# A two-layer streaming encoder on one core: another written order for TensorE (constants' products later, q k products two chunks ahead, samples' keys loaded early)

## The chip, the cores and the metric

The kernel runs on one core of one Trainium2 chip. The metric is the device time of one execution in microseconds (us). Engines are named as the profile names them: PE is TensorE (PEld its weight loads), DVE VectorE, ACT ScalarE, POOL GpSimd, SP the engine that issues the DMAs. L12 is line 12 of the kernel's file; where the change shifts lines, a line of the kernel before is meant unless the text says otherwise.

## What is computed

Two layers over 512 prompt frames (one stream) and 8 x 16 sample frames of running streams. Cut to what matters here:

```
def _hybrid_layer(x, ...):
    proj = _rms_norm(x, norm1) @ w_in          # u_a, g_a, u_b, q, k, v
    out_a = _rglru_mixer(u_a, g_a, ...)        # conv of width 4, two gates, scan
    out_b = _s5_mixer(u_b, ...)                # complex state space, scan
    q, k = _rope(q), _rope(k)
    out_c = _swa_prompt(q, k, v, sinks)        # prompt: chunks of 64, window of 3 chunks
          # or _swa_cached(q, k, v, cache_k, cache_v, sinks) for the samples
    x = x + concat([out_a, out_b, out_c]) @ w_out
    return x + square(relu(_rms_norm(x, norm2) @ w_up)) @ w_down
```

Attention is 8 heads of 64 on 2 heads of keys; its softmax has a sink logit per head.

## The kernel before

The 640 columns (frames) are two groups g of 320: 256 prompt frames (four chunks cq of 64) and 64 sample frames. Products with the large weights come in units of 128 output rows: 8 blocks of 128 x 128, in two halves of 4. In the first projection (layer 0, g = 0) the weights are used as they are (L271, 8 products a unit); everywhere else a weight is split in two parts on ACT (L243) and DVE (L244), and a half is 12 products (L274, L275, L276).

Three mixers run beside these products, for each layer and group: LRU ("L"), S5 ("S") and attention ("A"). Each is a Python generator; a string TURNS says whose turn is next, and `weave(M, n, A, m)` writes n turns of the mixers between m halves of products. So the order on PE is written out by hand, in the order in which Python calls it. The orders on DVE, ACT, POOL and SP are made when the program is built, by a scheduler that simulates the program; each engine then runs its list in order.

PSUM banks come from small pools: three for the large products ("mm"), two for attention and the LRU's gates ("att"), two for S5 ("s5"), one for norms ("fin"). A tile of a pool waits until the tile that had its place has been read for the last time.

The places that the prediction's steps touch:

- The start: products on zeros (L1156), the first input's norm (`first(0)`, with L374 and L411 on PE), then the constants of S5: `lru_const` and `s5_small` (L429 to L515, small DVE operations), `s5_const` with complex products on DVE and POOL (L520 to L526) into the tile tab, transposes of tab on PE (L176, into banks s), products L570, and tables by doubling (L589 to L611).
- S5: transposes of ub, copies L808 and L815, products with B (L822), evacuation against the tables (L829), scan (L840), then products L855, L858 and at last L886.
- LRU: conv (L750), gates (L759 on PE, L760 on ACT), scans (L776), the product with the gate (L781 and L782 on POOL).
- Attention: `own` transposes the samples' values (L176, att<-vS; copied by L921), `sprobs` has the samples' q k products (L952) and their softmax, `sturned` transposes these probabilities, `svalues` (L970) multiplies them with the values. `probs(cq)` has a chunk's q k products (L994) and softmax, `turned` the transposes, `values` the products with the values (L1015).
- `soft`: row maxima (L929), exponentials on ACT (L935), scaling on DVE and POOL (L945). `sprobs` and `probs` each take both att banks and give them back when the exponentials are done.

Of the kernel before, what the change touches and what calls it, by code (L numbers as in the profile page):

```python
# [14 lines left out]
AF = mybir.ActivationFunctionType  # L15
# [132 lines left out]
def encoder_kernel(ctx: ExitStack, tc: tile.TileContext, a, o):  # L148
    nc = tc.nc
    PE, V, S, G = nc.tensor, nc.vector, nc.scalar, nc.gpsimd  # L150
    mm = PE.matmul
    tt = V.tensor_tensor
    act = S.activation
# [20 lines left out]
    def transpose(out, in_):  # L174
        n = in_.shape[0]
        PE.transpose(out, in_, ident[0:n, 0:n])  # L176

    def bigr():
        return big.tile([128, 8, 2, NG], F32R, tag="big", name="bigr")
# [20 lines left out]
    W, n = {}, 0  # L200
# [16 lines left out]
    tab = cst.tile([128, 3840], F32, name="tab")  # L217
# [104 lines left out]
    def weave(steps, n, fill, m):  # L322

        done = 0
        for i in range(n):
            next(steps, None)
            while done < (i + 1) * m // n:
                next(fill, None)
                done += 1
# [563 lines left out]
            dma(o["send"][L], P["send"])  # L893


    def attention(L, P, g, q, mix, c):
        c, mix = c(), mix()

        kcT, p = c.at(0, 2, 2, 144), [c.at(640 + 288 * n, 2, 144) for n in range(2)]
# [2 lines left out]
        half = [slice(32 * n, 32 * n + 16) for n in range(2)]  # L902
        vn, pn = ([c.at(o, 2, 128)[h] for h in half] for o in (1792, 2048))

        pes = [c.at(640 * n, 2, 320) for n in range(2)]
        PTs = [c.at(1280 + 512 * n, 2, 256) for n in range(2)]
        kT, vt = kvs[L]["kT"], kvs[L]["vt"]

        def loads():
            for hf in range(2):  # L910
                dma(kcT[:, hf, :, 0:128], a["kc"][L, 2 * g + hf])
                dma(vc[:, hf], a["vc"][L, 2 * g + hf])
            gcopy(kcT[:, :, :, 128:144], q.kS.rearrange("p (h b t) -> p h b t", t=16, h=2))

        def own():
            b = bank3("att", 4, 128)[0:16]
            for hf in range(2):
                for i in range(2):
                    transpose(b[:, 2 * hf + i], q.vS[:, 16 * (2 * hf + i):16 * (2 * hf + i) + 16])
            for hf in range(2):  # L920
                V.tensor_copy(vn[hf], b[:, 2 * hf:2 * hf + 2])  # L921
# [25 lines left out]
        def sprobs():  # L947
            bs = [bank3("att", 2, 256) for hf in range(2)]
            for hf, b in enumerate(bs):
                for i in range(2):  # L950
                    for kv in range(2):
                        mm(b[64 * kv:64 * kv + 64, i, 0:144], lhsT=q.qS[64 * kv:64 * kv + 64, 2 * hf + i].rearrange("p i t -> p (i t)"),  # L952
                           rhs=kcT[64 * kv:64 * kv + 64, hf, i], start=True, stop=True)
            soft([b[:, :, 0:144] for b in bs], p, sks[:, L:L + 1], nsks[:, L:L + 1], True)
# [27 lines left out]
        def probs(cq):  # L982
            j, kts, nk, k0, st, w0 = geo(cq)
            q0 = 64 * cq
            if cq == 0:
                for pe in pes:
                    G.memset(pe[:, :, 0:64], 0.0)
                    G.memset(pe[:, :, 256:320], 0.0)
            bs = [bank3("att", 2, 256) for kv in range(2)]
            for pr in range(2):  # L990
                for s in range(2):
                    for kv, b in enumerate(bs):
                        ps = slice(64 * kv, 64 * kv + 64)
                        mm(b[64 * s:64 * s + 64, pr, 0:nk], lhsT=q.q[ps, 2 * pr + s, q0:q0 + 64], rhs=kT[ps, k0:k0 + nk], start=True, stop=True)  # L994
            soft([b[:, :, 0:nk] for b in bs], [pe[:, :, st:256] for pe in pes], skp[:, L], nskp[:, L], False)

        def turned(cq, kv):
            j, kts, nk, k0, st, w0 = geo(cq)
            b = bank("att").rearrange("p (t n q) -> p t n q", t=2, n=2)
            for kt in kts:  # L1000
                for n in range(2):
                    transpose(b[:, kt, n], pes[kv][:, n, w0 + 128 * kt:w0 + 128 * kt + 128])
            t0 = kts[0]
            src = b[:, t0:2].rearrange("p t n q -> p t (n q)")
            if kv == 0:
                act(PTs[kv][:, t0:2], src, AF.Copy)
            else:
                V.tensor_copy(PTs[kv][:, t0:2], src)

        def values(cq):  # L1010
            j, kts, nk, k0, st, w0 = geo(cq)
            b = bank("att")[:, 0:256]
            for kv in range(2):
                for kt in kts:
                    mm(b[64 * kv:64 * kv + 64, :], lhsT=vt[:, j - 1 + kt, 64 * kv:64 * kv + 64], rhs=PTs[kv][:, kt],  # L1015
                       start=kt == kts[0], stop=kt == 1)
            src = b.rearrange("p (i q) -> p i q", i=4)
            q0 = 64 * cq
            act(mix[:, 4:8, 0, q0:q0 + 64], src, AF.Copy)
            tt(mix[:, 4:8, 1, q0:q0 + 64], src, mix[:, 4:8, 0, q0:q0 + 64].bitcast(F32), OP.subtract)  # L1020

        loads()
        own()
        yield
        sprobs()
        yield
        sturned(0)
        yield
# [2 lines left out]
        svalues(0)  # L1031
        svalues(1)
        yield
        probs(0)
        for cq in range(4):
            yield
            for kv in range(2):
                turned(cq, kv)
            yield
            if cq < 3:  # L1040
                probs(cq + 1)
                yield
            values(cq)


    TURNS = "LSSLSSSS" "LAAAAAAA" + 5 * "AAS"

    def mixers(L, P, g, q, out, scratch=None):
        c = Carve(bigf() if scratch is None else scratch)
        mix = []  # L1050

        def gens(n):
            if not mix:
                mix.append(bigr())
            return mix[0]

        out["mix"] = gens
        ca = []

        def catt():  # L1060
            if not ca:
                ca.append(Carve(tp.tile([128, 2304], F32, tag="att", name="att")))
            return ca[0]

        G3 = {"L": lru(L, P, g, q, lambda: gens(0), c), "S": s5(L, P, g, q, lambda: gens(0), c),
              "A": attention(L, P, g, q, lambda: gens(0), catt)}
        for t in TURNS:
            next(G3[t], None)
            yield
        for v in G3.values():  # L1070
            assert next(v, "end") == "end"
# [77 lines left out]
    ctx.enter_context(tc.manual_schedule(engines={mybir.EngineType.PE}))  # L1149

    warm = bank("fin")
    zr = bigr()[:, 0:1].rearrange("p a b c -> p (a b c)")
    G.memset(tab[:, 512:1152], 0.0)
    act(zr, tab[:, 512:1152], AF.Copy)
    for n in 8 * (512,) + 4 * (512, 384):
        mm(warm[:, 0:n], lhsT=zr[:, 0:128], rhs=zr[:, 0:n], start=True, stop=True)  # L1156
    dma(sm[:, 0:80], a["sm"][:, 0:80])
    raws = first(0)
    P = {}
    q, m = [Proj(), Proj()], [{}, {}]  # L1160
    A = stream(in_proj(0, 0, norms[0], q[0], raws))
    weave(iter(()), 1, A, 4)
    dma(sm[:, 80:], a["sm"][:, 80:])
    first(1)
    small_prep()
    s5_small(lru_const())
    small = layer_small(0, P)
    next(small)
    weave(small, 2, A, 10)
    M = mixers(0, P, 0, q[0], m[0], setup[0])  # L1170
    weave(M, 8, A, 10)
    run(A)
    for L in range(DEPTH):
        last = L == DEPTH - 1
        A = stream(in_proj(L, 1, norms[1], q[1]))
        weave(M, 23 if L == 0 else 8, A, 16)
        run(M)
        M = mixers(L, P, 1, q[1], m[1])
        weave(M, 8, A, 8)
        run(A)  # L1180
        hm = {}
        F = stream(out_proj(L, 0, m[0], hm))
        weave(M, 7, F, 16)
        run(F)
        F = stream(mlp(L, 0, (0,), hm, fresh=(0,)))
        weave(M, 16, F, 28)
        run(M, F)
        run(stream(out_proj(L, 1, m[1], hm)))
        run(stream(mlp(L, 0, (1,), hm, fresh=(1,))))
        run(stream(mlp(L, 1, (0, 1), hm)))  # L1190
        run(stream(mlp(L, 2, (0, 1), hm)))
        nxt = (lambda g: Norm(g, None)) if last else (lambda g: Norm(g, n1(L + 1)))
        norms = {}
        F = stream(mlp(L, 3, (0,), hm, nxt, norms))
        if last:
            run(F)
            end = [norms[0].flush, lambda: finals(0)]
            items = mlp(L, 3, (1,), hm, nxt, norms)
            items[3:3] = end[:1]
            items[5:5] = end[1:]  # L1200
            run(stream(items))
        else:
            P = {}
            small = layer_small(L + 1, P)
            next(small)
            weave(small, 2, F, 24)
            run(F)
            q, m = [Proj(), Proj()], [{}, {}]
            A = stream(in_proj(L + 1, 0, norms[0], q[0]))
            weave(iter(()), 1, A, 14)  # L1210
            M = mixers(L + 1, P, 0, q[0], m[0])
            weave(M, 8, A, 10)
            run(A)
            F = stream(mlp(L, 3, (1,), hm, nxt, norms))
            weave(M, 15, F, 32)
            run(F)
# [27 lines left out]
```

## Time and profile before

| | |
|---|---|
| three runs | 1485.14, 1485.28, 1489.25 us (median 1485.28) |
| profiled execution | 1489.39 us, its span 1487.6 us |
| PE busy | 1377.3 us, 93% of the span |
| PE idle | 110.3 us |
| mean granted clock of PE | 0.959 of full speed |
| DVE, ACT, POOL busy | 881.3, 653.7, 356.0 us |

Busy times are sums over one profiled execution. A view with idle times names in brackets what ended them; when the engine named had finished long before, it was another. The 1.8 us between span and time lie outside of the profile's first and last instruction.

### The profile page before, as it was taken

What the parts mean: (1) busy time and instruction counts of PE and PEld (TensorE: products, weight loads), DVE (VectorE), ACT (ScalarE), POOL (GpSimd) and SP (SyncE); (2) the same over time, 40 slices, a digit from 0 to 9 for tenths busy, and PEclk for the clock granted to TensorE, in tenths of its full rate; (3) what the DMA queues carried; (4) which work ended last, traced back from release to release, by engine and by line L of the source; (5) the groups of instructions that cost most, each with busy time, mean ns of one, the idle gap of its engine ahead of it and who ended that gap; (6) DMA issues with size and microseconds to landing.
All of it is one profiled execution on the core that took longest, in us unless ns stands there. A gap on an engine that the chain in (4) does not pass through costs nothing.

```text
span 1487.6 us, 25403 instructions
## 1 busy us (share of the span) xinstructions
PE 1377.3 (93%) x9436; PEld 1315.2 (88%) x9436; DVE 881.3 (59%) x1726; ACT 653.7 (44%) x1348; POOL 356.0 (24%) x566
## 2 busy tenths in 40 slices
PE   4596896999999999999997999799999999999997
PEld 3465785989999999999996899699999999999997
DVE  7666677766644334336777677776664433434574
ACT  4155574545533223224575567654543322323543
POOL 4553248251101001006433223421100100100111
PEclk8796997999999999999998999899999999999998
DMA  6131232335432222224432333233443222223452
GB/s 214 38 111 36 68 116 81 98 118 163 143 128 71 80 78 71 77 87 128 144 117 79 104 119 117 83 106 114 147 144 122 71 72 80 77 71 107 149 177 93
DMA packets 91387, 156.24 MB, mean 105 GB/s; under 512 B 14336, under 2 KB 18304, under 8 KB 91264
## 3 DMA queue, kind: packets, MB, share of 16 engines
q1 hardware_dynamic: 91264, 154.63, 31.6%
q8 instruction: 74, 1.21, 0.3%
q14 instruction: 49, 0.40, 0.1%
HBM read 151.02 MB, written 3.37 MB: 104 GB/s over the span
## 4 chain that ended last, share of the span: by engine, by line
PE 85%; POOL 5%; DVE 4%; ACT 2%; issue 2%; DMA 1%; SPq 0%; DVEq 0%; POOLq 0%; ACTq 0%
PE mm L274 25%; PE mm L275 25%; PE mm L276 25%; PE mm L271 3%; PE att L176 1%; PE att L1015 1%; PE fin L411 1%; PE att L994 1%; PE s L176 1%; PE s L858 1%; PE s L886 1%; PE att L970 1%; DVE wl L244 1%; PE fin L374 1%; DMA raw<-w_in 1%
## 5 line engine op out<-in xcount | busy, mean ns | idle before, releaser
L274 PE MATMUL mm<-bigr,wh 128*128 128x320 f32 x2592 | 822.4, 317 | 2.3 <-POOL bigr L156 2.3
L275 PE MATMUL mm<-bigr,wh 128*128 128x320 f32 x2592 | 808.4, 312 | 0.9 <-DVE bigr L1091 0.9
L276 PE MATMUL mm<-bigr,wl 128*128 128x320 f32 x2592 | 808.0, 312 | 0.0
L243 ACT ACTIVATE wh<-raw 128x512 fp32r<-128x512 f32 x520 | 327.2, 631 | 517.6 <-PE mm L275 484.6
L274 PEld LDWEIGHTS mm<-bigr,wh 128*128 128x128 f32 x2592 | 494.3, 191 | 15.8 <-issue 8.3
L275 PEld LDWEIGHTS mm<-bigr,wh 128*128 128x128 f32 x2592 | 494.4, 191 | 2.2 <-DVE bigr L1091 1.3
L276 PEld LDWEIGHTS mm<-bigr,wl 128*128 128x128 f32 x2592 | 493.8, 190 | 0.0
L244 DVE TENSOR_TENSOR wl<-raw,wh 128x512 fp32r<-128x512 f32 x520 | 375.7, 723 | 179.8 <-ACT wh L243 168.4
L156 POOL TENSOR_SCALAR bigr<-t 128x320 fp32r<-128x320 f32 x128 | 59.7, 467 | 662.9 <-ACT t L1089 662.9
L1075 DVE TENSOR_TENSOR xT<-xT,mm 128x320 f32<-128x320 f32 x160 | 77.9, 487 | 133.6 <-PE mm L276 133.5
L1088 DVE SCALAR_TENSOR_TENSOR t<-mm,r 128x320 f32<-128x320 f32 x128 | 62.5, 491 | 94.2 <-PE mm L276 93.9
L1091 DVE TENSOR_TENSOR bigr<-t,bigr 128x320 fp32r<-128x320 f32 x128 | 66.0, 515 | 74.7 <-POOL bigr L156 74.6
L1089 ACT ACTIVATE t<-t 128x320 f32<-128x320 f32 x128 | 60.1, 472 | 111.0 <-DVE t L1088 105.3
L368 POOL TENSOR_TENSOR ss<-ss,sq 128x320 f32<-128x320 f32 x58 | 55.7, 960 | 184.5 <-ACT sq L361 178.8
L176 PE MATMUL att<-ident,att 128*128 128x128 f32 (+1 forms) x144 | 23.7, 301 | 40.9 <-DVE att L945 35.6
L176 PEld LDWEIGHTS att<-ident,att 128*128 128x128 f32 (+1 forms) x144 | 16.8, 143 | 44.9 <-issue 31.0
L945 POOL TENSOR_SCALAR att<-att,st 128x192 f32<-128x192 f32 (+3 forms) x40 | 33.0, 832 | 67.9 <-ACT wh L243 45.7
L935 ACT ACTIVATE att<-att,st 128x192 f32<-128x192 f32 (+3 forms) x80 | 30.6, 395 | 27.3 <-DVE st L933 20.9
L361 ACT ACTIVATE sq<-xT 128x320 f32<-128x320 f32 x66 | 30.5, 462 | 17.7 <-POOL ss L368 10.7
L348 ACT ACTIVATE bigr<-xT,sm 128x320 fp32r<-128x320 f32 x56 | 30.6, 561 | 11.3 <-DVE xT L1075 9.1
L690 POOL TENSOR_TENSOR sw<-sw,cs 128x320 f32<-128x320 f32 x20 | 17.5, 874 | 70.5 <-ACT sw L689 54.9
L349 DVE SCALAR_TENSOR_TENSOR bigr<-xT,sm,bigr 128x320 fp32r<-128x320 f32 x56 | 34.0, 615 | 0.5 <-ACT bigr L348 0.3
(291 smaller groups left out, 1070.2 us busy)
## 6 DMA issues: line engine op xcount, KB each, us to landing
raw<-w_up SPq DMA_DIRECT2D x192, 256.0 KB, 2.6
raw<-w_down SPq DMA_DIRECT2D x192, 256.0 KB, 2.6
raw<-w_in SPq DMA_DIRECT2D x85, 256.0 KB, 2.7
raw<-w_out SPq DMA_DIRECT2D x64, 256.0 KB, 2.6
wl<-w_in SPq DMA_DIRECT2D x11, 256.0 KB, 2.9
xT<-x SPq DMA_DIRECT2D x8, 320.0 KB, 5.7
yT<-xT SPq DMA_DIRECT2D x8, 320.0 KB, 2.9
cs<-rope SPq DMA_DIRECT2D x4, 320.0 KB, 3.3
```

The source lines that it names most:

```text
L156: return G.tensor_scalar(out, in_, 1.0, 0.0, OP.mult, OP.add)
L176: PE.transpose(out, in_, ident[0:n, 0:n])
L243: act(h, raw, AF.Copy)
L244: tt(l, raw, h.bitcast(F32), OP.subtract)
L274: mm(pt, lhsT=h[:, k % 4], rhs=m[:, k, 0], start=k == 0, stop=False)
L275: mm(pt, lhsT=h[:, k % 4], rhs=m[:, k, 1], start=False, stop=False)
L276: mm(pt, lhsT=l[:, k % 4], rhs=m[:, k, 0], start=False, stop=k == 7)
L368: G.tensor_tensor(self.ss, self.ss, sq, OP.add)
L1075: tt(xT[:, g, k], xT[:, g, k], pt, OP.add)
L1088: V.scalar_tensor_tensor(t, pt, 0.0, norm.r, OP.max, OP.mult)
L1089: act(t, t, AF.Square)
L1091: tt(am[:, f, 1], t, am[:, f, 0].bitcast(F32), OP.subtract)
```

## The change

It writes another order for PE, in five edits.

1. The start: 12 products of 128 x 128 on the zeroed tile Mm take the place of 16 products on a zeroed tile of their own. Only one unit is written ahead of the constants instead of two units; 15 more halves follow before the constants' transposes, and the second group's norm (`first(1)`) moves behind the constants.
2. Mixers of layer 0, g = 0: 9 turns between 4 halves instead of 8 between 10.
3. Attention: `loads` becomes a turn of its own and the first of all (TURNS now begins with A). `probs(0)` stands before `sturned(0)`, `probs(1)` behind `svalues`, and then a chunk's transposes come two chunks behind its q k products.
4. Two sets of probabilities (`sets`): chunks 0 and 2 use words 3200 to 4480 of the mixers' scratch tile, chunks 1 and 3 the old place. The LRU's x2 and t2 lie in the words 3200 to 4528 of the same tile.
5. TURNS and the counts of `weave` are fitted to the one turn more.

```diff
-    def attention(L, P, g, q, mix, c):
+    def attention(L, P, g, q, mix, c, cs):
...
-        pes = [c.at(640 * n, 2, 320) for n in range(2)]
+
+        sets = [[cs.at(3200 + 640 * n, 2, 320) for n in range(2)], [c.at(640 * n, 2, 320) for n in range(2)]]
...
-            if cq == 0:
+            pes = sets[cq % 2]
+            if cq < 2:
...
-                    transpose(b[:, kt, n], pes[kv][:, n, w0 + 128 * kt:w0 + 128 * kt + 128])
+                    transpose(b[:, kt, n], sets[cq % 2][kv][:, n, w0 + 128 * kt:w0 + 128 * kt + 128])
...
+        def turn(cq):
+            for kv in range(2):
+                turned(cq, kv)
+
         loads()
+        yield
         own()
         yield
         sprobs()
+        yield
+        probs(0)
         yield
         sturned(0)
...
-        probs(0)
+        probs(1)
+        yield
         for cq in range(4):
+            turn(cq)
             yield
-            for kv in range(2):
-                turned(cq, kv)
-            yield
-            if cq < 3:
-                probs(cq + 1)
+            if cq < 2:
+                probs(cq + 2)
                 yield
             values(cq)
-
-
-    TURNS = "LSSLSSSS" "LAAAAAAA" + 5 * "AAS"
+            yield
+
+
+    TURNS = "ALSSLSSSS" "LAAAAAA" + 5 * "SAA" + "A"
...
-    weave(iter(()), 1, A, 4)
+    weave(iter(()), 1, A, 2)
     dma(sm[:, 80:], a["sm"][:, 80:])
-    first(1)
     small_prep()
     s5_small(lru_const())
     small = layer_small(0, P)
     next(small)
-    weave(small, 2, A, 10)
+    first(1)
+    weave(iter(()), 1, A, 15)
+    weave(small, 2, A, 3)
     M = mixers(0, P, 0, q[0], m[0], setup[0])
-    weave(M, 8, A, 10)
+    weave(M, 9, A, 4)
```

On PE, at the start of the program, the transposes of tab (the constants) stand as follows in the difference; the products between (L271) are left out where they are many.

```order
 L271 MATMUL mm<-bigf,wl 128x320 x4
-L176 MATMUL s_386<-ident,tab 128x128 x4
-L176 MATMUL s_392<-ident,tab 128x128 x4
 L411 MATMUL fin<-ident,rsq 128x128 x2
 L411 MATMUL fin<-ident,rsq 128x64
...
+L176 MATMUL s_536<-ident,tab 128x128 x4
+L176 MATMUL s_542<-ident,tab 128x128 x4
+L271 MATMUL mm<-bigf,wl 128x320 x4
+L570 MATMUL s_575<-tab 128x32 x8
```

Before, they stood ahead of L411 and of 80 of the first projection's 96 products; now 68 of these 96 stand ahead of them: 16, then 44 in one run behind L411, then, behind the transposes of v, 8 more.

On DVE, in the same stretch of the changed kernel, the evacuations of the first projection stand between the last steps of the constants (t and kT belong to k, the t of L672 to v):

```order
L526 TENSOR_TENSOR tab<-tab 128x256
L699 TENSOR_TENSOR t<-mm,cs 128x320
L520 TENSOR_TENSOR tab<-s5s,tab 128x256
L525 TENSOR_TENSOR tab<-s5s,tab 128x256
L522 TENSOR_TENSOR tab<-tab 128x16x16
L700 TENSOR_TENSOR kT<-t,sw 128x256
L701 TENSOR_TENSOR kS<-t,sw 128x64
```

Before, all of the constants' steps stood ahead of L699.

On PE, in the first mixers' attention, the part from the samples' q k products to the transposes of their probabilities, in the difference (what is left out are products L274 to L276):

```order
-L952 MATMUL att<-att,qS 64x144 x8
...
+L953 MATMUL att<-att,qS 64x144 x8
...
+L996 MATMUL att<-kT,q 64x64 x8
 L176 MATMUL att<-ident,att 128x128
 L176 MATMUL att<-ident,att 16x128
```

The q k products of chunk 0 (L996, before L994) came to stand between the two. Before, 12 products stood between L952 and the transposes in this pass; in the later three passes 24. Now 12 stand before L996 and none behind it in this pass; in layer 1, g = 0, 24 and 24; in the two passes of g = 1, 24 and 36.

## Rows read from the trace of the kernel before

**Rows 1.** The profile's page: busy time of each engine, share of the span, instructions.

```profile
PE 1377.3 (93%) x9436; PEld 1315.2 (88%) x9436; DVE 881.3 (59%) x1726; ACT 653.7 (44%) x1348; POOL 356.0 (24%) x566
```

**Rows 2.** Waits of PE: line, awaited; us in total, times, longest.

```profile
PE att L176 <- DVE att L945: 35.6, 6, 10.7
PE s L176 <- DVE tab L522: 27.2, 1, 27.2
PE att L952 <- issue: 10.3, 3, 5.5
```

**Rows 3.** A window of 50 us: busy time of PE, PEld, DVE, ACT, POOL; clock, DMA.

```profile
400.00:450.00 50.00, 50.00 (x343) 50.00 (x342) 26.92 (x45) 18.03 (x30) 2.90 (x7) 1.00 0.39 127
```

**Rows 4.** PE in time, layer 0: start, duration, what, [idle before].

```profile
52.44 1.94 PE L176 MATMUL s<-ident,tab 128*128 128x128 f32 x8 [27.20 <-DVE tab L522]
...
61.19 2.32 PE L271 MATMUL mm<-bigf,raw 128*128 128x320 f32 x8
63.34 2.32 PE L271 MATMUL mm<-bigf,wl 128*128 128x320 f32 x8
...
67.65 1.87 PE L570 MATMUL s<-tab 128*128 128x32 f32 x16
...
102.73 1.11 PE L822 MATMUL s<-bigf,Bm 64*128 64x80 f32 x14 [0.66 <-DVE bigf L829]
...
113.95 1.01 PE L176 MATMUL att<-ident,vS 128*16 128x128 f32 x4 [4.49 <-ACT bigf L760]
```

**Rows 5.** DVE in time, start of layer 0.

```profile
36.26 0.84 DVE L525 TENSOR_TENSOR tab<-s5s,tab 128x256 f32<-128x256 f32 x1
...
49.49 0.42 DVE L525 TENSOR_TENSOR tab<-s5s,tab 128x256 f32<-128x256 f32 x1
...
62.41 3.10 DVE L750 SCALAR_TENSOR_TENSOR bigf<-uap,sm,bigf 128x332 f32<-128x332 f32 x6 [9.15 <-ACT bigf L748]
69.91 0.19 DVE L590 TENSOR_TENSOR tab<-tab 128x16 f32<-128x16 f32 x1 [4.39 <-POOL tab L156]
...
84.49 0.83 DVE L609 COPY tab<-s5s 128x1280 f32<-128x1280 f32 x1
```

**Rows 6.** PE in time, attention of layer 0, g = 1.

```profile
224.37 0.71 PE L952 MATMUL att<-att,qS 64*64 64x144 f32 x8 [3.13 <-issue]
240.99 0.66 PE L176 MATMUL att<-ident,att 128*128 128x128 f32 x2 [10.65 <-DVE att L945]
244.07 0.69 PE L176 MATMUL att<-ident,att 128*128 128x128 f32 x2 [2.43 <-POOL att L945]
```

**Rows 7.** SP, DVE, ACT and POOL in time, the same pass.

```profile
187.61 0.60 SPq L229 DMA_DIRECT2D att<-vc  x1
...
223.44 0.83 DVE L921 COPY att<-att 16x256 f32<-16x256 f32 x2
...
237.68 0.39 ACT L935 ACTIVATE att<-att,st 128x144 f32<-128x144 f32 x1
...
242.13 1.26 POOL L781 TENSOR_TENSOR bigf<-bigf,ga 128x512 f32<-128x512 f32 x1
```

**Rows 8.** PE in time, further waits in attention.

```profile
144.42 1.21 PE L176 MATMUL att<-ident,att 128*128 128x128 f32 x4 [3.78 <-DVE att L945]
...
154.38 0.65 PE L1015 MATMUL att<-att,vt 128*64 128x256 f32 x4 [1.44 <-ACT att L935]
...
176.51 1.26 PE L1015 MATMUL att<-att,vt 128*64 128x256 f32 x8 [2.31 <-ACT att L935]
...
799.24 1.11 PE L176 MATMUL att<-ident,att 128*128 128x128 f32 x4 [5.58 <-DVE att L945]
...
946.90 0.66 PE L176 MATMUL att<-ident,att 128*128 128x128 f32 x2 [7.28 <-DVE att L945]
```

**Rows 9.** ACT in time: last exponentials of the samples, layer 1, both groups.

```profile
796.58 0.39 ACT L935 ACTIVATE att<-att,st 128x144 f32<-128x144 f32 x1
...
944.70 0.39 ACT L935 ACTIVATE att<-att,st 128x144 f32<-128x144 f32 x1
```

More of the change, by code (lines that the diff above doesn't have):

```diff
@@ L1065, in mixers @@
         G3 = {"L": lru(L, P, g, q, lambda: gens(0), c), "S": s5(L, P, g, q, lambda: gens(0), c),
-              "A": attention(L, P, g, q, lambda: gens(0), catt)}
+              "A": attention(L, P, g, q, lambda: gens(0), catt, c)}
         for t in TURNS:
@@ L1151, in encoder_kernel @@
     warm = bank("fin")
[L1152 to L1156, printed above, removed]
+    for _ in range(12):
+        mm(warm[:, 0:128], lhsT=Mm[:, 0:2].rearrange("p a b c -> p (a b c)"), rhs=Mm[:, 0:2].rearrange("p a b c -> p (a b c)"), start=True, stop=True)
     dma(sm[:, 0:80], a["sm"][:, 0:80])
@@ L1178, in encoder_kernel @@
         M = mixers(L, P, 1, q[1], m[1])
-        weave(M, 8, A, 8)
+        weave(M, 9, A, 8)
         run(A)
@@ L1211, in encoder_kernel @@
             M = mixers(L + 1, P, 0, q[0], m[0])
-            weave(M, 8, A, 10)
+            weave(M, 9, A, 10)
             run(A)
```

## Prediction

> **What bounds the kernel now.** I read the page's head first: PE is busy for 1377.3 of the span's 1487.6 us [rows 1], and the large products fill it, so what an order can win lies in PE's 110 us of idle time. The waits of PE say where these are [rows 2]: 27.2 us are one wait for the constants, 35.6 us are six waits for scaled probabilities (DVE L945), 10.3 us stand before the samples' q k products (L952). In the windows, a stretch of large products alone shows no idle time at all, 343 products in 50 us, so 12 cost 1.75 us [rows 3]. Last I read the waits' places in order of time on each engine [rows 4 to 9]: PE waits for chains over DVE, ACT and POOL, and moving PE's work helps only as far as the chain stays where it is.
>
> **Part by part: the start.** PE finishes its second unit at 25.25 us (52.44 less 27.20) and idles until tab is ready [rows 4]. Now 52 more of the first projection's products stand there. Half a unit costs 2.15 us (61.19 to 63.34), 4.3 us a unit. After L411 (1.6 us) five units, 21.5 us, take PE to 48.4. The sixth's bank is k's, and k's evacuation stands on DVE behind nearly all of the constants. These end at 52.3 in the trace; the group before the last is at 49.5 [rows 5]. Six conv operations that DVE did later (3.1 us, at 62.41) now stand ahead as well. I put k's evacuation at 52.5: PE waits 4 us, then 1.5 more for v's, three steps further down the same list. L570 then ends at 66.7 instead of 69.5 (half a unit, v's transposes, a unit, the constants' transposes of 1.94, half a unit, L570 itself). The tables follow L570 and took from 69.91 to 85.3; three evacuations of q stand ahead of them, so I put their end at 84. The copies for S5's product with B stand behind the tables on DVE; PE is there at 80 and waits 4.4. The second product with B follows with nothing between and waits 2 us for its banks; it ends at 90. From there to the transposes of vS the trace has 10.1 us (103.84 to 113.95); I take 8.7, since ACT's list has two evacuations less in between. They come at 98.7 instead of 113.95 [rows 4]. **Gain 15 us**, not 27: of the wait of 27.20 some 12 come back in five places. Ends: nothing (the chain over DVE takes as long as before, 113.95 again) and 27.
>
> The start's 12 products against 16 cost nothing either way: behind them PE idles for 3.6 us in any case, for the first norm.
>
> **The keys' early load.** The transfers of the samples' keys and values are issued by 188.2 already, and L952's second half runs at 224.37 [rows 6, 7]. What ended its wait is DVE's L921, from 223.44 to 224.27: it frees the att bank of the values' transposes. An earlier transfer gains 0, and the 10.3 us stay. On SP the loads wait for the old att tile, with weights queued behind; four raw tiles are ahead, which covers that.
>
> **Chunk 0's q k products behind the samples'.** They take 0.8 us and two att banks, which the samples' products hold until their exponentials are done. So PE waits there instead. In layer 0, g = 1: L952 ends at 225.1, 24 products run, L996 can start at about 237.5, since the last exponential ends at 238.1 [rows 7], then 36 products (5.3) run to 244; the transposes need the half that POOL scales, which came at 244.07 [rows 6]. The end stays within a microsecond, and 36 products and L996, 6.1 us, now lie inside the old 13.1 us of waiting. **Gain 5 us** (ends 0 and 6.1). In layer 1, g = 1, the exponentials end at 945.1, only 1.8 us before the transposes start [rows 8, 9], so 36 products end later against them: **gain 4**. In layer 1, g = 0, only 24 products follow L996, and 12 have moved ahead of S5: L996 starts at 796.5, behind the exponentials [rows 9], the transposes at 803 instead of 799.24 [rows 8]; 4 us more work in 4 us more time, **gain 0**, and 2 for the wait before chunk 0's transposes that goes. In layer 0, g = 0, nothing stands between L996 and the transposes, and these need the bank that chunk 0's exponentials give back: about 1.5 us more waiting, as many as stay hidden: **0**.
>
> **Two chunks ahead.** Of the waits 3.78, 1.44 and 2.31 in the first pass [rows 8] only the first goes. The others stand where PE wants an att bank 12 products (1.75 us) after q k products took both. The new order has this three times in that pass (chunk 1 to transposes of 0, chunk 2 to values of 0, chunk 3 to values of 1), at about 1.5 each: 7.5 becomes 4.5, **gain 3** (ends 0 and 7.5). A second set of probabilities adds no bank.
>
> The Trainium skill says of such repeating gaps ("Perfetto Trace Analysis", Identifying Performance Opportunities) that they can mean there isn't enough SBUF or PSUM for the next tile. Here it is PSUM: the wait at 154.38 ends with ACT's last exponential, as the page would have it. By it, the new SBUF set wins none of the 4.5 us that I leave; were the set what was short, the sum would be 4.5 more.
>
> **The new scratch.** Chunk 0's exponentials write over x2 and t2, so they wait for the LRU's scan and for POOL's L781 (242.13 to 243.4). The first two, which free the first bank, need only the scan. I take 0; the cover is 9 us of products until the next transposes.
>
> **Sum.** 15 + 5 + 4 + 2 + 0 + 3 = 29 us off 1489.4 (the profiled time): 1460. The median of the runs shown is 4.1 lower, so I predict 1485.3 - 29 = **1456 us**.
>
> **Rivals.**
> - *The holes close wholly.* If the evacuations get ahead of the constants on DVE and the banks come back early: 27 + 6 + 6 + 4 + 5 = about 45, so 1441. For it: DVE is busy for long but in small pieces. Against it: its list is fixed, and k's evacuation stands where it stands.
> - *The constants get longer.* DVE's steps cost 0.84 us beside POOL's and 0.42 alone [rows 5]. Now POOL's share of the constants and its share of the evacuations fall together. If the last 26 steps all cost 0.84, tab comes 11 us later, and the tables with it: 4 us left of 15, so 1467. For it: POOL's list has cs, uap and ub ahead of its steps. Against it: DVE's steps are not made longer by ACT, and half of them already cost this. The Trainium skill ("SBUF - State Buffer", two separate sides) calls the port that DVE and POOL share an exclusive lock: an operation of DVE with two inputs waits for POOL's whole instruction. The two durations agree with it.
> - *No change.* The start's chain ends at 113.95 again, since the tables, not PE, set it, and attention's gains shrink to a few us: 1481 to 1485. Against it: conv, gates and ub no longer wait for PE at 55.
> - *Slower.* One mechanism: in each of four passes the last exponential of chunk 0 stands in ACT's list until POOL has done L781, and the copies of weights (L243) behind it. PE has some four halves in hand, 7 us. If L781 comes more than 15 us behind p in all four passes, each loses 8, 33 in all: the gain is gone and the time over 1490. In the trace it is 2 us behind p [rows 6, 7].
>
> **How the numbers follow.** The forecast has 0.62 (its own range 1448 to 1466), wholly closed 0.15, longer constants 0.13, no change 0.06, slower 0.04. The range of 8 in 10 takes in the forecast, most of the second case and of the third: 1441 to 1470. It holds the ends of the start's gain but for 0 and 27 with everything else on the same side. Something like 0.3% (4.5 us) is what a measurement can tell: faster 0.90, same 0.06, slower 0.04.
>
> **What would show it.** PE idle for no more than 5 us at any place before 70 us, with k's evacuation as the releaser near 50; the constants' transposes near 60 with no wait; the tables' copy (L609) near 84 and a wait before the first product with B; the transposes of vS at 96 to 101. L952 still with waits of 2 to 5 us in its middle. A wait of 6 to 9 us before L996 in the passes of g = 1, released by ACT's exponentials, and next to none before the samples' transposes. Waits of 1 to 2 us before L1017 twice in the first pass. It is wrong if the vS transposes come near 114 (constants), near 87 (holes closed), or if products L274 wait for ACT's L243 in the attention stretches.

## The result and the profile after

| | before | after |
|---|---|---|
| time, median (range) | 1485.21 us (1484.62 to 1489.25, 4 runs) | 1453.18 us (1451.25 to 1453.52, 4 runs) |
| ratio, 95% interval | | 0.9776 (0.9757 to 0.9795) |
| profiled execution, its span | 1489.39 us, 1487.6 us | 1452.91 us, 1451.1 us |
| PE busy, PE idle | 1377.3 us, 110.3 us | 1374.8 us, 76.3 us |

The changed kernel takes 32.0 us less by the medians. The two profiled executions lie 36.5 us apart; a second profile of the kernel before, below, shows that some 5 of these belong to the first profile alone.

In the new file L952 has become L953, L994 L996, L1015 L1017 and L945 L946. The page's line of busy times, which answers to [rows 1]:

```profile
PE 1374.8 (95%) x9444; PEld 1313.1 (90%) x9444; DVE 882.4 (61%) x1726; ACT 651.5 (45%) x1347; POOL 360.0 (25%) x581
```

PE's busy time has hardly changed; 34.0 us of its idle time went. The waits of PE, which answer to [rows 2] (us in total, times, longest):

```profile
PE att L996 <- ACT att L936: 19.1, 6, 5.9
PE att L953 <- issue: 10.3, 3, 5.5
PE s L822 <- DVE bigf L815: 5.2, 1, 5.2
PE s L822 <- DVE bigf L829: 4.4, 7, 1.3
```

The 27.2 us for the constants and the 35.6 us for scaled probabilities (DVE L945) are both gone. In their place PE waits 19.1 us before q k products, for exponentials that hold the att banks, and in the first mixers' pass still 3.2 us before the samples' transposes, now for chunk 0's exponentials. The 10.3 us before the samples' products stand there to the tenth.

The start, PE in order of time (start, duration, what, [idle before]), answers to [rows 4]:

```profile
50.20 2.42 PE L271 MATMUL mm<-bigf,raw 128*128 128x320 f32 x8 [2.51 <-DVE t L699]
55.37 0.69 PE L176 MATMUL att<-ident,t 128*128 128x128 f32 x2 [2.75 <-DVE t L672]
...
61.49 1.04 PE L176 MATMUL s<-ident,tab 128*128 128x128 f32 x8
...
64.52 1.87 PE L570 MATMUL s<-tab 128*128 128x32 f32 x16
...
85.06 2.39 PE L822 MATMUL s<-bigf,Bm 64*128 64x80 f32 x16 [5.23 <-DVE bigf L815]
88.74 0.71 PE L822 MATMUL s<-bigf,Bm 64*128 64x80 f32 x2 [1.29 <-DVE bigf L829]
89.85 1.99 PE L822 MATMUL s<-bigf,Bm 64*128 64x80 f32 x14 [0.39 <-DVE bigf L829]
91.77 4.54 PE L271 MATMUL mm<-bigf,wl 128*128 128x320 f32 x8
...
100.30 1.01 PE L176 MATMUL att<-ident,vS 128*16 128x128 f32 x4 [2.87 <-ACT bigf L760]
```

In place of the one long wait stand four short ones: for k's evacuation (L699), for v's (L672), for the copies ahead of the products with B (L815) and for the next evacuations (L829, 1.29 and 0.39 us where [rows 4] have 0.66). The wait for ACT before vS was there before and has shrunk from 4.49 us to 2.87. DVE's rows give the reason of the third: the copies of L815 stand on DVE behind nearly all of the table code, of which L601 is the last step but for the copy at L609.

```profile
82.95 0.66 DVE L601 TENSOR_TENSOR tab<-tab 128x496 f32<-128x496 f32 x1
...
84.53 0.87 DVE L815 COPY bigf<-s 128x320 f32<-128x320 f32 x2
85.33 0.81 DVE L609 COPY tab<-s5s 128x1280 f32<-128x1280 f32 x1
```

Attention of layer 0, g = 1, PE in order of time, which answers to [rows 6]:

```profile
202.88 1.23 PE L953 MATMUL att<-att,qS 64*64 64x144 f32 x8 [3.15 <-issue]
...
215.80 2.27 PE L996 MATMUL att<-kT,q 64*64 64x192 f32 x16 [5.88 <-ACT att L936]
...
225.35 0.60 PE L176 MATMUL att<-ident,att 128*128 128x128 f32 x4
```

The samples' transposes (225.35) no longer wait; the 10.65 and 2.43 us of before have become 5.88 before L996.

### The profile page after: what moved, and what is told of

The parts are those of the page before. It is cut to its first block, busy times and chain, and to the rows that moved or that the text cites. A ratio compares the mean times of both kernels' runs of the same rounds, so it can differ in the third digit from the quotient of the medians.

```text
span 1451.1 us, 25432 instructions
## 1 busy us (share of the span) xinstructions
PE 1374.8 (95%) x9444; PEld 1313.1 (90%) x9444; DVE 882.4 (61%) x1726; ACT 651.5 (45%) x1347; POOL 360.0 (25%) x581
## 4 chain that ended last, share of the span: by engine, by line
PE 84%; DVE 7%; POOL 3%; ACT 2%; issue 2%; DMA 2%; SPq 0%; DVEq 0%; ACTq 0%; POOLq 0%
PE mm L274 26%; PE mm L275 25%; PE mm L276 25%; PE att L176 1%; PE att L1017 1%; PE s L858 1%; PE att L996 1%; PE fin L411 1%; PE s L886 1%; PE att L971 1%; PE s L822 1%; DVE wl L244 1%; DMA raw<-w_in 1%; PE s L176 0%; PE fin L374 0%
## 5 line engine op out<-in xcount | busy, mean ns | idle before, releaser
L274 PE MATMUL mm<-bigr,wh 128*128 128x320 f32 x2592 | 820.1, 316 | 1.6 <-POOL bigr L156 1.6
L276 PE MATMUL mm<-bigr,wl 128*128 128x320 f32 x2592 | 806.1, 311 | 1.1 <-DVE wl L244 1.1
L243 ACT ACTIVATE wh<-raw 128x512 fp32r<-128x512 f32 x520 | 327.4, 631 | 508.5 <-PE mm L275 479.4
L274 PEld LDWEIGHTS mm<-bigr,wh 128*128 128x128 f32 x2592 | 492.1, 190 | 15.5 <-issue 8.8
L276 PEld LDWEIGHTS mm<-bigr,wl 128*128 128x128 f32 x2592 | 491.9, 190 | 1.4 <-DVE wl L244 1.4
L244 DVE TENSOR_TENSOR wl<-raw,wh 128x512 fp32r<-128x512 f32 x520 | 377.0, 726 | 190.1 <-ACT wh L243 179.7
L996 PE MATMUL att<-kT,q 64*64 64x192 f32 (+2 forms) x256 | 16.6, 347 | 19.1 <-ACT att L936 19.1
L271 PE MATMUL mm<-bigf,raw 128*128 128x320 f32 x104 | 32.2, 456 | 2.5 <-DVE t L699 2.5
L996 PEld LDWEIGHTS att<-kT,q 64*64 64x64 f32 x256 | 9.4, 147 | 24.1 <-ACT att L936 21.3
L271 PEld LDWEIGHTS mm<-bigf,raw 128*128 128x128 f32 x104 | 20.3, 201 | 10.9 <-DVE t L699 3.0
```

The lines of the kernel that those rows point to most:

```text
L243: act(h, raw, AF.Copy)
L244: tt(l, raw, h.bitcast(F32), OP.subtract)
L271: mm(pt, lhsT=self.w[n][:, k % 4], rhs=m[:, k], start=k == 0, stop=k == 7)
L274: mm(pt, lhsT=h[:, k % 4], rhs=m[:, k, 0], start=k == 0, stop=False)
L276: mm(pt, lhsT=l[:, k % 4], rhs=m[:, k, 0], start=False, stop=k == 7)
```

## The experiments

All times are medians; the ratio is to runs of the kernel before on the same chip. The runs come from three chips, on which the kernel before had medians of 1484.98, 1485.80 and 1486.55 us, and the intervals are some 2 us to either side; so I estimate that a difference between two runs of this table is good to about 3 us. "Halves" are halves of a unit of large products. The mixers run in four passes: layer 0 with g = 0 and g = 1, then layer 1 with both. Lengths are read from the profile between the first transposes of ub and of vS in each pass; "the first pass from vS" ends at the ub of the second, and the second and third pass are taken from ub to the next pass's ub.

| run | us | ratio (95%) |
|---|---|---|
| start_alone | 1474.26 | 0.9924 (0.9908 to 0.9940) |
| s_early | 1462.86 | 0.9850 (0.9833 to 0.9867) |
| chunk0_late | 1468.15 | 0.9880 (0.9867 to 0.9893) |
| one_ahead | 1453.07 | 0.9777 (0.9763 to 0.9790) |
| s_late | 1456.78 | 0.9801 (0.9788 to 0.9814) |
| keys_late | 1452.10 | 0.9773 (0.9760 to 0.9786) |
| attention_alone | 1467.62 | 0.9875 (0.9862 to 0.9888) |
| const_2_earlier | 1451.36 | 0.9762 (0.9749 to 0.9776) |
| turned_s5 | 1459.77 | 0.9810 (0.9794 to 0.9826) |
| more_fill | 1458.88 | 0.9815 (0.9801 to 0.9828) |
| milder_fill | 1452.70 | 0.9776 (0.9760 to 0.9792) |
| before_again | 1483.88 | one run |

**before_again.** The kernel before, unchanged, with a second profile.

> The kernel before the change, once more with a profile, since its profiled execution lay 4.1 us above the median. If that is spread over the run (weights that come late, a wait here and there), its stages up to the fourth pass agree with the first profile within 2 us each, and the time is 1484 to 1488 us; if it lies in the first pass, the gain that I read from the two profiles there is too large by as much.

The stages of this profile in the first layer (window, length, PE busy, clock, DMA share, GB/s):

```profile
80.30:111.55 31.25, 26.23 (x130) 0.96 0.31 103
111.55:190.02 78.47, 62.84 (x470) 0.84 0.20 63
```

The transposes of vS come at 111.55, not 113.95 as in [rows 4]; the first pass has the same length within 0.3 us. In the third pass, between vS and ub, this profile has 123.05 us and the first had 126.50. So 2.4 us of the start and 3.4 of the third pass belong to the first profile alone, which is neither of the two cases that I expected: these two stages differ by more than 2 us, but the first pass does not. Below, the stages are compared with this second one.

**start_alone and attention_alone.** The two halves of the change, each alone on the kernel before. The first takes the 12 warm products and these lines of the start:

```diff
-    weave(iter(()), 1, A, 4)
+    weave(iter(()), 1, A, 2)
...
+    first(1)
+    weave(iter(()), 1, A, 15)
-    weave(small, 2, A, 10)
+    weave(small, 2, A, 3)
...
-    weave(M, 8, A, 10)
+    weave(M, 8, A, 4)
```

The second takes all of attention and TURNS, on the old start:

```diff
-    weave(M, 8, A, 10)
+    weave(M, 9, A, 10)
```

> The kernel before with the start alone of the changed one: the twelve warm products, the constants' products behind 17 and 20 halves of the first projection, the second group's input read after the constants' code; attention and its turns are as before. By my theory (the changed kernel's gain is the sum of a start that is worth 13 to 15 us and of an attention that is worth the rest, some 18) it takes 1470 to 1472 us, 13 to 15 less than before. The first rival is that the 4.4 us by which TensorE was busy for less time in the rest of the first pass (after vS) also come from the start, through the granted clock: then 1466 to 1468. The second is that the two parts do not add up, because a start without the new attention turns only moves the idle time to the first transposes of vS: then above 1476.

> The changed kernel with the start of before (the long warm products, the constants' products behind 4 + 5 and 4 + 10 halves, the second group's input early); attention and turns are the changed ones. By my theory the four passes of attention are worth, read from the changed profile, 3.4 us of idle time in the first pass, 5.1 in the second, 4 to 7 in the third and 3 in the fourth: 1466 to 1470 us. If the 4.4 us of busy time in the first pass and the 2.9 in the third, which I did not foresee, belong to the attention too, it comes to 1465 or a little under; if they belong to the start, 1470 or more.

The start is worth 11.5 us, under what I expected, and the attention with its turns 18.2; together 29.7 of the 32.0. They add up within what the runs can tell. The profile of the start alone shows where it gave less: from vS on the first pass is longer than before (78.47 us, 62.84 of them busy), and that almost wholly in busy time. First the start alone, then the changed kernel:

```profile
100.12:182.92 82.80, 66.62 (x471) 0.77 0.19 60
```

```profile
100.30:171.29 70.99, 59.31 (x471) 0.89 0.19 64
```

The six runs of the start alone spread from 1471.45 to 1478.10 us, and the profile is of one with 1477.08, so not every run need lose so much here. PE in windows of this pass (vS stands at 100.12 and at 100.30), first the start alone, then the changed kernel:

```profile
100.00:110.00 10.00, 6.91 (x44) 0.83 0.16 51
110.00:120.00 10.00, 4.47 (x19) 0.51 0.08 26
120.00:130.00 10.00, 9.63 (x69) 0.50 0.08 26
130.00:140.00 10.00, 6.97 (x45) 0.63 0.09 29
140.00:150.00 10.00, 8.04 (x65) 0.83 0.16 52
```

```profile
110.00:120.00 10.00, 4.67 (x31) 0.50 0.08 28
120.00:130.00 10.00, 10.00 (x95) 0.83 0.17 55
130.00:140.00 10.00, 9.01 (x88) 1.00 0.15 52
```

After the wait around 110 both run at a granted clock of 0.50, the lower level (1.2 GHz). In the changed kernel it is back at 1.00 from 130 on; with the start alone a second wait comes near 130 and the clock is 0.63. PE is busy from 120 to 130 in both, but gets through 69 and 95 instructions.

**s_early.** What gave the first pass its gain? One thing more than the start alone:

```diff
-    TURNS = "LSSLSSSS" "LAAAAAAA" + 5 * "AAS"
+    TURNS = "LSSLSSSS" "LAAAAAA" + 5 * "SAA" + "A"
```

> The run with the start alone (attention as before the change: chunk 0 behind the samples' values, one chunk ahead, one set of probabilities), with one thing more: the list of turns puts each of the last five s5 turns two attention turns earlier, the first behind the products over the samples' values, where the changed kernel has it. Since the run with chunk 0 late and the one with one chunk ahead both kept the first pass's gain, and the start alone did not have it, I now hold the place of the s5 turns to be what is worth 8 to 11 us in the first pass: they are work for TensorE while chunk 0's exponentials run. Then it takes 1464 to 1469 us. If instead either two chunks ahead or the early chunk 0 is enough by itself for that gain and the s5 turns' place is worth nothing, 1472 to 1476.

1462.86: on top of the start the string of turns is worth 11.4 us (11.0 by the ratios), a little more than expected. Its first pass, PE in order of time from the samples' transposes to those of chunk 0, ahead of it the second wait of the start alone:

```profile
133.03 1.20 PE L176 MATMUL att<-ident,att 128*128 128x128 f32 x4 [3.41 <-DVE att L945]
```

```profile
114.59 0.66 PE L176 MATMUL att<-ident,att 128*128 128x128 f32 x2 [7.68 <-DVE att L945]
...
127.09 0.79 PE L855 MATMUL s<-Mm,bigf 64*80 64x64 f32 x16
127.81 1.36 PE L858 MATMUL s<-Cm,bigf 128*80 128x64 f32 x16
...
131.82 0.60 PE L176 MATMUL att<-ident,att 128*128 128x128 f32 x4
```

The samples' wait stays at 7.68. The s5 products (L855, L858) now run while chunk 0's exponentials do, and the second wait is gone. From vS to the next pass it takes 69.97 us, against 82.80 with the start alone and 78.47 before: by the profiles some 4 of these 12.8 us only give back what the start alone had lost there.

**chunk0_late and one_ahead.** Each takes one part of the new attention order away from the changed kernel; with s_early, which lacks both, and the changed kernel, which has both, they fill a square. (s_early also lacks the second set of probabilities and the early load; the other three have both.) First chunk 0 late, then one chunk ahead, both against the changed kernel:

```diff
-        probs(0)
-        yield
         sturned(0)
...
+        probs(0)
+        yield
         probs(1)
```

```diff
-        probs(1)
-        yield
         for cq in range(4):
             turn(cq)
             yield
-            if cq < 2:
-                probs(cq + 2)
+            if cq < 3:
+                probs(cq + 1)
```

> The changed kernel with the q k products of chunk 0 moved back behind the products over the samples' values, right ahead of those of chunk 1; all else as changed. My theory prices their early place at 5 us in each pass of the second group and at 2 to 4 in the third pass: 1464 to 1468 us, 11 to 15 more than the changed kernel, with the wait for the samples' exponentials back ahead of the samples' transposes (line 176). The rival is that two chunks ahead does the work and the place of chunk 0 is worth little, since its products only wait for a bank earlier: 1453 to 1457.

> The changed kernel with chunk 0 in its new place, behind the samples' products, but each later chunk's q k products one chunk ahead only: chunk 1 after the transposes of chunk 0, as before the change. My prediction priced two chunks ahead at 3 us, all in the first pass, and the run with chunk 0 late put about 7 us of the first pass down to the turns as a whole: so 1456 to 1461 us, with the loss between the transposes of vS of the first pass and the next pass, and almost none in the second and fourth passes. The rival is that the place of chunk 0 alone gives the first pass its 7 us and that two chunks ahead is worth nothing: 1452 to 1454.

| | one chunk ahead | two chunks ahead |
|---|---|---|
| chunk 0 behind the samples' values | 1462.86 | 1468.15 |
| chunk 0 behind the samples' q k products | 1453.07 | 1453.18 |

Chunk 0's early place is worth 9.8 us with one chunk ahead, 15.0 with two (10.8 and 15.4 by the ratios). Two chunks ahead wins nothing that the runs can tell where chunk 0 is early, and costs 5.3 (4.5 by the ratios) where it is late. So my theory of some 3 us for it falls, and so does the rival of the first of these runs, that it does the work; the time of the second run is its rival's. The waits of the run with chunk 0 late:

```profile
PE att L176 <- DVE att L946: 31.8, 4, 10.7
PE att L953 <- issue: 10.2, 3, 5.5
```

These are the old waits of [rows 2] but for two of the six. Against the changed kernel the profile of this run is 0.8 us longer in the first pass from vS, 6.3 in the second pass, 3.2 in the third and 5.4 in the fourth.

**s_late.** The reverse of s_early: the changed kernel with the s5 turns back at the end.

```diff
-    TURNS = "ALSSLSSSS" "LAAAAAA" + 5 * "SAA" + "A"
+    TURNS = "ALSSLSSSS" "LAAAAAA" "AAAS" + 4 * "AAS"
```

> The changed kernel with the last five s5 turns three attention turns later in the list, the last at its end as before the change; chunk 0 early and two chunks ahead stay. If the s5 turns' place is what the first pass gained by, it loses 6 to 11 us there: 1459 to 1465 us, with a new wait of 3 us or more before the transposes of the probabilities of chunk 0 in the first pass. If the early chunk 0 with two chunks ahead gains it in any case, 1451 to 1455.

It loses 3.6 us, between the two expectations, and not where I looked for it: from vS to the next pass the first pass takes 70.36 us (70.99 in the changed kernel); 2.9 us go in the second pass and 1.5 in the third. So in the first pass the s5 turns' place and the early chunk 0 are two covers for one wait, and either is enough: 69.97 us with the first alone, 70.36 with the second, 70.99 with both, 82.80 with neither (78.47 on the old start).

**keys_late.** The early load undone:

```diff
         loads()
-        yield
         own()
...
-    TURNS = "ALSS...
+    TURNS = "LSS...
```

> The changed kernel without the early load: the samples' keys and values are asked for in the same turn as the transposes of vS again, and the extra first turn is gone from the list. My theory says that the load was already hidden, since the first products over the samples' keys wait for a bank that VectorE gives back and not for the DMA: 1452 to 1455 us, the same as the changed kernel within 0.2%. The rival, that the early load is what shortened the passes of the third and fourth (7.0 and 3.0 us), gives 1459 to 1463, and a wait of over 2 us before the products at line 953 that ends with a DMA.

1452.10, within 0.1% of the changed kernel, and the wait at line 953 is the same 10.3 us, three times, longest 5.5. The rival, that the early load shortened the third and fourth passes, falls.

**const_2_earlier.**

```diff
-    weave(iter(()), 1, A, 15)
-    weave(small, 2, A, 3)
+    weave(iter(()), 1, A, 13)
+    weave(small, 2, A, 5)
```

> The changed kernel with the constants' transposes two halves earlier (behind 13 halves, not 15) and the sixteen products at line 570 three halves earlier ahead of the rest: the count of halves is the same. If the wait of 5.2 us ahead of the first B product is the tables' lateness on VectorE (they cannot begin before the products at line 570 have read the region they are written to), it goes almost wholly: 1447 to 1450 us. If the table code is held up by something else, or the transposes now wait for the constants' last products on VectorE (they end near 56), 1452 to 1455, with a new wait of 1 to 4 us ahead of the transposes near 57.

1451.36, 1.8 us less, which the intervals don't tell from nothing. The edit did less than I wrote: L570 moved by one half, not three. PE in this run:

```profile
56.15 1.97 PE L176 MATMUL s<-ident,tab 128*128 128x128 f32 x8
57.91 4.22 PE L271 MATMUL mm<-bigf,wl 128*128 128x320 f32 x8
...
64.12 1.87 PE L570 MATMUL s<-tab 128*128 128x32 f32 x16
```

The transposes stand right behind the waits for k and v and take 1.97 us instead of 1.04, the half behind them 4.22 instead of 2.32; L570 comes 0.4 us earlier than in the changed kernel. The wait before the first B product is 2.71 instead of 5.23, but PE also came there later, and the product itself starts at 85.48, not before the 85.06 of the changed kernel; whether an earlier table removes the wait stays open.

**turned_s5.** Two more banks for the transposes of the probabilities:

```diff
-            b = bank("att").rearrange("p (t n q) -> p t n q", t=2, n=2)
+            b = bank("s5").rearrange("p (t n q) -> p t n q", t=2, n=2)
```

> The changed kernel with the transposes of the probabilities written to the two banks of the s5 stage instead of the two of attention, so that the turns of the chunks no longer wait for the bank that the next chunk's exponentials hold. By my theory (with two chunks ahead the banks are short, not the set of probabilities) the waits before the probabilities' transposes and the values go, 2 to 6 us, most of it in the first pass: 1447 to 1452 us. The rival is that the s5 stage needs its banks at the same turns and waits instead: 1452 to 1458.

The rival's side holds, past its range: 6.6 us slower (5.0 by the ratios). PE in the first pass of this run:

```profile
135.74 0.35 PE L855 MATMUL s<-Mm,bigf 64*80 64x64 f32 x2 [0.52 <-DVE att L1010]
137.11 0.82 PE L855 MATMUL s<-Mm,bigf 64*80 64x64 f32 x14 [1.01 <-ACT att L1008]
...
156.16 0.65 PE L1017 MATMUL att<-att,vt 128*64 128x256 f32 x4 [1.30 <-ACT att L936]
```

The s5 products now wait for the copies of the transposes (L1008, L1010), and the values still wait, since they kept the att bank. The first pass behind vS takes 74.11 us instead of 70.99. The second pass is 4.3 us longer too; its cause I did not trace.

**more_fill and milder_fill.** More large products where PE waits, fewer behind; first the stronger fill, against the changed kernel:

```diff
-        weave(M, 7, F, 16)
+        for steps, halves in ((1, 0), (1, 4), (1, 5), (1, 3), (3, 4)):
+            weave(M, steps, F, halves)
...
-            weave(M, 15, F, 32)
+            for steps, halves in ((1, 1), (1, 5), (1, 4), (12, 22)):
+                weave(M, steps, F, halves)
```

The milder one has the second piece, the constants as in const_2_earlier, and for the first piece

```diff
+        for steps, halves in ((1, 1), (1, 3), (1, 3), (1, 3), (3, 6)):
```

> The changed kernel with the same products spread unevenly over the attention's turns in the last three passes: four to five halves instead of two behind the transposes of vS and behind the samples' q k products, fewer behind the later turns. If the waits ahead of lines 953 and 996 (10.3 and 13.5 us in those passes) are only a shortage of large products between the turns, most of them go: 1437 to 1444 us. If the banks' round trip sets the pace (a bank is taken, held by the exponentials and given back), the waits move behind the next turns and the gain is under 4 us: 1449 to 1453.

> The changed kernel with the constants' transposes two halves earlier, in the third pass the uneven spread of the run that filled the waits (there its stage was 2.0 us shorter), and in the second and fourth pass one half more behind the transposes of vS alone, taken from ahead of them, with 3, 3, 3 and then 6 halves over the three last turns. If VectorE's weight splits and the banks made the stronger fill slow, this one keeps clear of them: 1445 to 1450 us. If any product moved forward comes back as a wait behind it, 1451 to 1455.

The stronger fill is 5.7 us slower than the changed kernel, outside both expectations; the milder one is the same as the changed kernel, as its second expectation had it. Waits of PE with the stronger fill:

```profile
PE mm L276 <- DVE wl L244: 12.3, 9, 3.9
PE att L971 <- DVE att L963: 8.2, 3, 5.3
...
PE att L996 <- ACT att L936: 5.9, 3, 5.5
```

The waits that it aimed at went: L953 fell from 10.3 to 0.4, L996 fell from 19.1 to 5.9. But the products moved forward wait for DVE's split of their weights (L244), and the samples' values (L971), now with fewer products ahead, wait for a copy on DVE. The waits were not a shortage of products alone; DVE was as late.

## Why the prediction was right, and where its steps were not

The time, 1453.18, lies 2.8 us under the 1456 predicted. The terms, against the second profile of before (spans 1482.1 and 1451.1, so 31.0 us); the last three rows are taken from one pass's first transposes of ub to the next's, or to the end:

| step | predicted | in the profiles |
|---|---|---|
| start, up to vS | 15 | 11.3 (111.55 to 100.30) |
| first pass behind vS | 3 | 7.5 (78.47 to 70.99) |
| layer 0, g = 1 | 5 | 4.9 |
| layer 1, g = 0 | 2 | 3.5 |
| layer 1, g = 1 | 4 | 3.9 |

Between the third and the fourth row 1.75 us are moved, for the 12 products that the new turns put ahead of the third pass: 20.60 us from L411 to the transposes of ub before, 22.35 after. The sum fits better than its terms: the start came out some 4 us short, 2.4 of them by the choice of profile, and the first and third passes won 4.5 and 1.5 more than was said. That they cancel is luck.

**The start** went as written and was over-sized. k's evacuation had PE wait 2.51 us (predicted 4) and v's 2.75 (1.5); L570 ended at 66.4 (66.7), the tables' copy ran at 85.33 (84), the first B product waited 5.23 (4.4) and the second 1.7 (2). The vS transposes were to come at 98.7 and came at 100.30. The missing term is the clock. In the changed kernel it was granted at 0.50 here (window, length, PE busy, clock, DMA share, GB/s):

```profile
85.00:96.00 11.00, 9.26 (x40) 0.50 0.14 48
```

The products with B took 2.39, 0.71 and 1.99 us where the kernel before has

```profile
98.22 1.12 PE L822 MATMUL s<-bigf,Bm 64*128 64x80 f32 x16
...
101.63 0.45 PE L822 MATMUL s<-bigf,Bm 64*128 64x80 f32 x2
```

and 1.11 [rows 4]: 2.4 us together, more than the 1.6 us by which vS comes late. The half at 91.77 took 4.54 us instead of 2.32 as well, but that did not delay vS. The transposes of vS wait for ACT's L760, which stands on ACT behind L842. That waits for DVE's scan (L840), and the scan for POOL's L831, which stands on POOL behind L837 (93.74 to 95.06), which works on what the last products with B gave:

```profile
95.15 2.85 DVE L840 TENSOR_TENSOR_SCAN bigf<-tab,bigf 128x640 f32<-128x640 f32 x1 [0.98 <-POOL bigf L831]
```

```profile
98.10 1.49 ACT L842 ACTIVATE bigf<-bigf 64x640 f32<-64x640 f32 x2 [4.44 <-DVE bigf L840]
99.61 0.54 ACT L760 ACTIVATE bigf<-att,hcols 128x332 f32<-128x332 f32 x1
```

From the end of the products with B to vS it took 8.5 us (predicted 8.7). Another 2.4 us lie in the profile that I summed against. Of the rivals for the start, closed holes would have had vS near 87; longer constants were to show near 114, though their own price, 11 us on 98.7, gives some 110; neither came. In the list of PE's waits in the changed kernel none ends with ACT's L243, the sign of the slower case.

**Chunk 0's place** was right in mechanism and near in size: 5 and 4 predicted in the two passes of g = 1, 4.9 and 3.9 in the profiles, 6.3 and 5.4 when it alone is taken back (chunk0_late), and 9.8 us in all for the place with one chunk ahead. The wait before L996, released by ACT's exponentials, was there, but shorter than the 6 to 9 us that were said: 5.88 and, in the fourth pass, 4.89 us; before the samples' transposes there was none. Their end did not stay within a microsecond: in layer 0, g = 1 they end 31.0 us behind vS, 28.3 before, since from 215.80 to 225.40 us the clock was granted at 0.66 and L996 took 2.27 us, not 0.8, and the 36 products some 7.4, not 5.3. In layer 1, g = 0 the prediction's 803 us does not follow from its own terms (796.5, L996 with 0.8 and 24 products with 3.5 make 800.8); the transposes did come at about that distance from vS (25.65 us, 26.05 by the prediction), because the 24 products took 5.1 us at a clock of 0.73.

**Two chunks ahead, gain 3,** is the step that failed. No run shows a gain: 1453.07 us without it, 1453.18 with it, and the first pass, where all of it was to lie, says more than the medians. From the samples' transposes to the second pass, first the changed kernel, then one_ahead:

```profile
116.50:171.29 54.79, 51.52 (x411) 0.94 0.21 69
```

```profile
116.58:169.90 53.32, 51.56 (x411) 0.93 0.22 71
```

The busy time is the same, and the idle time is 3.3 us with two chunks ahead and 1.8 with one: the 7.5 us of waits for att banks did shrink, more than to the 4.5 that were said, but not by this step.

What I had passed over is the string of turns, which the prediction does not price at all: on top of the start it is worth 11.4 us, on top of all the rest 3.6 (s_late). The prediction also put chunk 0's place at 0 in the first pass, where it is the second cover for the same wait. The first pass gained 7.5 us because TensorE got other work in the second of two waits that followed each other, and 3.5 of them are busy time (62.84 to 59.31 for the same instructions but one), as the clock came back sooner (0.84 and 0.89 over the pass). The sum came out because this unpriced gain stood in for the 3 us and for what the start lacked.

**The reading that banks, not the set of probabilities, are short.** The prediction took up the Trainium skill ("Perfetto Trace Analysis", Identifying Performance Opportunities), which says that a repeating gap can mean too little SBUF or PSUM, and chose PSUM for the gaps that it left. The trace agrees in so far as the waits before L1017 still end with exponentials (ACT L936: 3.8 us, three times, and 1.4 once). That two more banks would mend it did not hold as I built it (1459.77). That the second set wins nothing is not shown: every run with chunk 0 early has it. By the code it is what makes that place possible: the samples' probabilities lie in words 640 to 1216 of the attention tile, inside the old place of the chunks' (0 to 1280), so chunk 0's exponentials could not have been written there before the samples' transposes, and those need an att bank that chunk 0 holds until its exponentials are done.

**The keys' early load, 0,** is shown by keys_late. One sum among the rivals is off: 27 + 6 + 6 + 4 + 5 is 48, not 45, so that wholly closed holes would have meant 1437 us, under the range's lower end. The 12 or 16 first products and the waiting of chunk 0's exponentials for POOL's L781 were not run by themselves.

## What to carry to other kernels

When PE waits twice in a row for two softmaxes, one cover is enough; here an independent stage (s5) moved by two turns gave it, or the next q k products moved forward. Price every piece of the order, the string of turns too, not only the edits that have a name. A wait costs its idle time and then the slower products behind it, so sum a stage in busy time as well as in idle time, and count the slower products only where what waits next depends on them. Moving large products into a wait pays only as long as the engine that prepares their operands is ahead: look at its waits before more are moved.

## What the hardware showed that I had not expected

- The granted clock stayed low behind short waits: in the changed kernel's start PE waited 5.23 us and then 1.29 and 0.39 us, the clock was 0.50 from 85 to 96 us, and a half of large products took 4.54 us instead of 2.32; with the start alone the clock was 0.50 from 120 to 130 us, though PE was busy for 9.63 of these 10 us.
- Two executions of one kernel differed by 2.4 us in the start and 3.4 us in the third pass and by 0.3 us in the first pass: a sum of stages should be made against more than one profile.
